# A masked prefix sum and its product on one core: taking the leftover rows behind the first two loads of a round, and transposing the sums in quarters

## The chip, the cores and the metric

The kernel runs on one core of a Trainium2 chip. The metric is the device time of one execution in microseconds (us), as the median of several runs. Most executions agree within a few tenths of a per cent (84.34 to 84.82 us in the fourteen runs of behind_one_warm, below). Some take longer (86.0 us in the profiled run of the kernel before), and a run over 1.5% above the fastest of its kernel is labelled slow.

Ratios are the mean time of one kernel's fast runs over that of the other's from the same rounds, so a ratio is not quite the ratio of the medians quoted beside it.

## The reference

```python
mask = (pos < lengths[:, None, None]).astype(np.float32)
cs = np.cumsum(x * mask, axis=1)              # x: 8 x 8192 x 512, f32
mid_features = cs[b_idx, lengths // 2, :]     # one row for each batch entry
return np.matmul(mid_features[:, None, :], w).squeeze(1)
```

Only one row of the cumulative sum is used, so each batch entry needs the sum of its first min(length, length/2 + 1) rows, times a 512x512 matrix. Those are 570, 2690, 256, 2057, 905, 3772, 3859 and 571 rows. The kernel reads 31.2 MB, hardly more than these rows and `w`.

## The kernel before

The rows are summed by TensorE: a block of 512 rows (128 partitions, four rows each, 1 MB) is multiplied by 0/1 weights and added to PSUM. Whole blocks go through three buffers of two blocks each, the *places* of a round; a round takes three places (two blocks are loaded ahead of the rounds and one, the last, behind them). What is left of each batch entry (fewer than 512 rows) is its *rest*. There are two buffers for rests, and two rests are taken in each of the first four rounds, which are all the rounds that these lengths need. SyncE requests the places' loads, ScalarE the rests' loads, each when the buffer is free again. VectorE prepares the weights of the next round, and only then is a buffer free.

The three pieces that matter, the round on TensorE first:

```python
with pe.Fori(0, rounds):
    with pe.If_cmp(rest_rounds, 1, "IS_GE"):
        for q in range(2):                                  # the two rests of this round
            take(pe, s_rem[q], 16 * (len(PARTS) + 1))       # wait for its loads
            for j in range(G):
                mm = add(j, cur_rem[:, q, j * B:(j + 1) * B], rem[:, q, j])
            mm.then_inc(s_rdone[q], 1)                      # through VectorE, lets ScalarE request the next

    def add_pair(k):
        keep_busy()                                         # three filler matmuls
        take(pe, s_full[k], 32)                             # wait for the place's loads
        ...                                                 # second block, if there is one
        for j in range(G):
            mm = add(j, cur[:, k, 0], xt[:, k, 0, j])
        mm.then_inc(s_done[k], 1)                           # through VectorE, lets SyncE request the next

    pairs(pe, left, add_pair)                               # places 0, 1, 2
```

The fillers (`keep_busy`) are matmuls whose result nobody reads; they are meant to keep TensorE's clock up (in after_cold, below, which has none ahead of the second place, that place of the last round ran at half clock, 3.60 us instead of 1.90). After the last round the sums are copied to SBUF, folded and, with the last block's rows, added up by column (in three pieces, so that the last load is met by little work), transposed by VectorE in two halves, and multiplied by `w`:

```python
for h in range(2):                                          # VectorE
    step(dve.transpose, out=t_sb[:, 2 * h:2 * h + 2].rearrange("p k c -> p (k c)"),
         in_=t_ps[:, :P].rearrange("p (c k) -> p k c", k=KC)[:, 2 * h:2 * h + 2])
...
for kc in range(KC):                                        # TensorE
    if kc % 2 == 0:
        pe.wait_ge(s_dve, DVE_ALL + 3 + kc // 2)
    for j in range(4):
        mm = pe.matmul(o_ps[32 * j:32 * j + B, :P], lhsT=t_sb[:, kc, :B], ...)
```

## Time and profile before

| | before |
|---|---|
| median time | 84.55 us (84.5 to 84.6, 3 runs) |
| the profiled run | 86.0 us, labelled slow |
| span in the profile | 84.1 us |
| read from HBM | 31.23 MB |

The page has a row of digits for each engine: the busy share, in tenths, of each fortieth of the span. The DMA row stands at 9 for nearly the whole kernel, TensorE's (PE) does not. So I take it that the loads set the pace, and that what TensorE does matters only where it delays a load or stands behind the last one. The lines are shown in the prediction; what it calls the ring of an engine are the loads that the engine has requested and that are still to land.

### The profile page before, as it was taken

The numbers are of one execution on the slowest core, as the hardware profiler recorded it, in microseconds if no ns is written. First come the engines' busy times: TensorE is split into PE (matmuls) and PEld (weight loads), VectorE is DVE, ScalarE is ACT, GpSimd is POOL, SyncE is SP. The second block draws the span as 40 slices with busy tenths as digits, with TensorE's granted clock in tenths as the row PEclk, the third lists the DMA queues.
The fourth block names the chain that finished last, engine by engine and source line by source line (L and its number), as shares of the span: only waits on it lengthen the run. The fifth ranks groups of instructions, "written<-read, shape, count | busy, mean of one in ns | idle before, by whom it ended". The sixth has DMA issues, their size and how long they took to land. (4 is left out here: it accounts for less than half of the span.)

```text
span 84.1 us, 1482 instructions
## 1 busy us (share of the span) xinstructions
PE 57.5 (68%) x385; PEld 12.9 (15%) x389; DVE 15.2 (18%) x79; ACT 5.5 (7%) x6; POOL 1.6 (2%) x13
## 2 busy tenths in 40 slices
PE   2950799759980499999406932899979729099730
PEld 2300111112210112121101200111122111023410
DVE  2858887000000000100000010000000000001420
ACT  2991000000000000000000000000000000000020
POOL 6100000000000000000000000000000000000000
PEclk9999999999999555899995696557999999999999
DMA  3799999999999999999999999999999999996000
GB/s 55 288 421 417 441 428 438 445 405 437 417 433 413 421 429 405 421 444 405 452 429 386 441 431 435 398 417 456 415 380 429 429 413 425 402 322 234 6 8 8
DMA packets 3540, 31.26 MB, mean 372 GB/s; under 512 B 531, under 2 KB 547, under 8 KB 1203
## 3 DMA queue, kind: packets, MB, share of 16 engines
q1 hardware_dynamic: 2610, 27.27, 77.5%
q10 hardware_dynamic: 928, 3.97, 12.4%
q8 instruction: 1, 0.02, 0.1%
q14 instruction: 1, 0.00, 0.0%
HBM read 31.23 MB, written 0.02 MB: 372 GB/s over the span
## 5 line engine op out<-in xcount | busy, mean ns | idle before, releaser
L492 PE MATMUL s_ps<-xt,cur 128*8 128x512 f32 x184 | 26.4, 699 | 12.6 <-PEq L146 12.5
L505 PE MATMUL idle_ps<-idle 128*128 128x512 bf16 x44 | 15.3, 443 | 4.0 <-DVE since L340 3.6
L492 PE MATMUL s_ps<-rem,cur_rem 128*8 128x512 f32 x64 | 10.0, 725 | 4.4 <-PEq L146 4.4
L492 PEld LDWEIGHTS s_ps<-xt,cur 128*8 128x8 f32 x184 | 4.3, 95 | 27.7 <-issue 27.7
L456 DVE TENSOR_TENSOR cur<-since 128x16 f32 x9 | 1.7, 187 | 35.6 <-DVEq L146 35.6
L505 PEld LDWEIGHTS idle_ps<-idle 128*128 128x128 bf16 x48 | 3.7, 104 | 21.6 <-issue 20.1
L310 ACT COPY o_sb<-o_ps 8x128 f32<-8x128 f32 x2 | 0.5, 260 | 74.1 <-PE o_ps L586 74.1
L261 ACT ACTIVATE rem<-rem 128x2048 uint32<-128x2048 uint32 x2 | 3.7, 1902 | 0.0
L492 PEld LDWEIGHTS s_ps<-rem,cur_rem 128*8 128x8 f32 x64 | 1.8, 104 | 11.7 <-issue 11.7
L464 DVE COPY cur_rem<-table 128x32 f32 x6 | 1.1, 181 | 11.9 <-DVEq L146 11.9
L516 PE MATMUL s_ps<-zero 1*128 1x512 f32 x2 | 2.1, 1136 | 1.6 <-DVE zero L340 1.6
L340 DVE COPY s_sb<-s_ps 128x256 f32<-128x256 f32 x2 | 0.8, 424 | 12.6 <-PE idle_ps L509 12.6
L492 PE MATMUL s_ps<-first,cur_first 128*8 128x512 f32 x16 | 3.0, 824 | 0.0
L498 PE MATMUL t_ps<-last,e_last 128*8 128x128 f32 x32 | 1.6, 274 | 0.0
L586 PE MATMUL o_ps<-wt,t_sb 128*8 128x128 f32 x32 | 1.1, 273 | 0.5 <-DVE t_sb L340 0.5
L261 ACT ACT_TABLE_LOAD x1 | 1.3, 1283 | 1.4 <-PEq L607 1.4
L340 DVE TENSOR_TENSOR part_a<-since,step_a 1x42 f32<-1x42 f32 (+1 forms) x2 | 1.1, 560 | 0.1
L586 PEld LDWEIGHTS o_ps<-wt,t_sb 128*8 128x8 f32 x32 | 0.8, 89 | 0.7 <-issue 0.7
L340 DVE TENSOR_TENSOR since<-item,begin 1x42 f32<-1x42 int32 (+1 forms) x2 | 0.8, 422 | 0.1
L519 PEld LDWEIGHTS n_ps<-len_f,ones 1*128 1x128 f32 x2 | 0.7, 332 | 1.0 <-DVE len_f L340 0.5
L498 PEld LDWEIGHTS t_ps<-last,e_last 128*8 128x8 f32 x32 | 0.7, 88 | 0.7 <-DMA last<-in_x_dram 0.6
L498 PE MATMUL t_ps<-s_sb,fold 128*8 128x128 f32 x8 | 0.8, 274 | 0.0
(66 smaller groups left out, 13.3 us busy)
## 6 DMA issues: line engine op xcount, KB each, us to landing
xt<-in_x_dram SPq DMA_DIRECT2D x10, 2048.0 KB, 11.7
xt<-in_x_dram SPq DMA_DIRECT2D x3, 1024.0 KB, 10.4
first<-in_x_dram SPq DMA_DIRECT2D x2, 1024.0 KB, 8.0
rem<-in_x_dram ACTq DMA_DIRECT2D x3, 512.0 KB, 8.6
wt<-in_w_dram ACTq DMA_DIRECT2D x1, 1024.0 KB, 4.9
rem<-in_x_dram ACTq DMA_DIRECT2D x3, 256.0 KB, 9.1
last<-in_x_dram SPq DMA_DIRECT2D x1, 512.0 KB, 9.3
last<-in_x_dram SPq DMA_DIRECT2D x2, 256.0 KB, 9.5
```

What stands on the lines that cost most here:

```text
L261: act.memzero(rem[:, q]).then_inc(s_rfree[q], 1)
L310: copy = act.copy(out=o_sb[1][:, j * P:(j + 1) * P], in_=o_ps[64 + 32 * j:64 + 32 * j + B, :P])
L340: do(*args, **kw).then_inc(s_dve, 1)
L456: dve.tensor_tensor(out=cur[:, k], in0=since[:, :B, here].rearrange("p b h -> p h b"), in1=since[:, 1:, here].rearrange("p b h -> p h b"), ...
L464: dve.tensor_copy(out=cur_rem[:, q], in_=rests[:, ds(dve.snap(of, min_val=1, max_val=B // 2 - 1), 1), q].rearrange("p o w -> p (o w)"),).t ...
L492: return pe.matmul(s_ps[32 * j:32 * j + B], lhsT=weights, rhs=rows, start=False, stop=False, skip_group_check=True, tile_position=(0, 32 * j))
L498: return pe.matmul(t_ps[32 * j:32 * j + B, :P], lhsT=weights, rhs=row[:, P * j:P * (j + 1)], start=False, stop=False, skip_group_check=Tru ...
L505: pe.matmul(idle_ps[:], lhsT=idle[:, :P], rhs=idle[:], start=True, stop=True)
L516: pe.matmul(s_ps[:], lhsT=zero[:], rhs=zero[:, :1].to_broadcast((1, D)), start=True, stop=False, skip_group_check=True)
L519: pe.matmul(n_ps[:, :B], lhsT=ones[:], rhs=len_f[:], start=True, stop=True).then_inc(s_pe, 1)
L586: mm = pe.matmul(o_ps[32 * j:32 * j + B, :P], lhsT=t_sb[:, kc, :B], rhs=wt[:, kc, j * P:(j + 1) * P], start=(kc == 0), stop=(kc == KC - 1) ...
```

## The change

Its intent: TensorE shall not stand waiting for rests at the start of a round while the first place has already landed, so that buffers come free earlier; and the product shall start after a quarter of the transposes instead of a half. The diff, cut to its core (VectorE's loop gets the same order):

```diff
         with pe.Fori(0, rounds):
-            with pe.If_cmp(rest_rounds, 1, "IS_GE"):
-                for q in range(2):
-                    take(pe, s_rem[q], 16 * (len(PARTS) + 1))
-                    ...
             def add_pair(k):
                 ...
-            pairs(pe, left, add_pair)
+            pairs(pe, left, add_pair, 0, NS - 1)            # places 0 and 1
+            with pe.If_cmp(rest_rounds, 1, "IS_GE"):
+                for q in range(2):
+                    take(pe, s_rem[q], 16 * (len(PARTS) + 1))
+                    ...
+            pairs(pe, left, add_pair, NS - 1)               # place 2
...
-        for h in range(2):
-            step(dve.transpose, out=t_sb[:, 2 * h:2 * h + 2]..., in_=...)
+        for k in range(KC):
+            step(dve.transpose, out=t_sb[:, k], in_=t_ps[:, :P].rearrange("p (c k) -> p k c", k=KC)[:, k])
...
             for kc in range(KC):
-                if kc % 2 == 0:
-                    pe.wait_ge(s_dve, DVE_ALL + 3 + kc // 2)
+                pe.wait_ge(s_dve, DVE_ALL + 3 + kc)
```

More of the change, by code (lines that the diff above doesn't have):

```diff
@@ L146, in take, with pairs @@
         eng.wait_ge(s, n).then_inc(s, -n)
-    def pairs(eng, n, body, k=0):
-        if k < NS:
+    def pairs(eng, n, body, k=0, most=NS):
+        if k < most:
             with eng.If_cmp(n, 2 * k + 1, "IS_GE"):
                 body(k)
-                pairs(eng, n, body, k + 1)
+                pairs(eng, n, body, k + 1, most)
     def rounds_of(eng, n, least):
@@ L171 @@
     DVE_SEL, DVE_ADDR, DVE_N, DVE_FIRST, DVE_MASK, DVE_ALL = 2, 15, 6, 32, 49, 58
-    DVE_LAST = DVE_ALL + 6
+    DVE_LAST = DVE_ALL + 2 + KC + 2
     PE_ALL, PE_SUM, PE_OUT = 2, 3, 4
@@ L459, in weights @@
                 ).then_inc(s_free[k], 1)
+            pairs(dve, left, weights, 0, NS - 1)
             with dve.If_cmp(rest_rounds, 1, "IS_GE"):
@@ L467, in _ @@
                     ).then_inc(s_rfree[q], 1)
-            pairs(dve, left, weights)
+            pairs(dve, left, weights, NS - 1)
             less(dve, rest_rounds, 1)
@@ L478, in _ @@
         dve.wait_ge(s_pe, PE_SUM)
-        for h in range(2):
-            step(dve.transpose, out=t_sb[:, 2 * h:2 * h + 2].rearrange("p k c -> p (k c)"),
-                 in_=t_ps[:, :P].rearrange("p (c k) -> p k c", k=KC)[:, 2 * h:2 * h + 2])
+        for k in range(KC):
+            step(dve.transpose, out=t_sb[:, k], in_=t_ps[:, :P].rearrange("p (c k) -> p k c", k=KC)[:, k])
         with ending(dve, "dve_last", hint):
@@ L534, in _ @@
         with pe.Fori(0, rounds):
-            with pe.If_cmp(rest_rounds, 1, "IS_GE"):
-                for q in range(2):
-                    take(pe, s_rem[q], 16 * (len(PARTS) + 1))
-                    for j in range(G):
-                        mm = add(j, cur_rem[:, q, j * B:(j + 1) * B], rem[:, q, j])
-                    mm.then_inc(s_rdone[q], 1)
             def add_pair(k):
@@ L550, in add_pair @@
                 mm.then_inc(s_done[k], 1)
-            pairs(pe, left, add_pair)
+            pairs(pe, left, add_pair, 0, NS - 1)
+            with pe.If_cmp(rest_rounds, 1, "IS_GE"):
+                for q in range(2):
+                    take(pe, s_rem[q], 16 * (len(PARTS) + 1))
+                    for j in range(G):
+                        mm = add(j, cur_rem[:, q, j * B:(j + 1) * B], rem[:, q, j])
+                    mm.then_inc(s_rdone[q], 1)
+            pairs(pe, left, add_pair, NS - 1)
             less(pe, left, PER)
```

## The prediction

> **What bounds the kernel now.** I read the page first: the busy tenths by slice, the DMA part and the chain of waits; then the timeline of the last 13 us; then busy times in chosen stretches.
>
> ```profile
> span 84.1 us, 1482 instructions
> ...
> PE   2950799759980499999406932899979729099730
> ...
> PEclk9999999999999555899995696557999999999999
> DMA  3799999999999999999999999999999999996000
> ...
> HBM read 31.23 MB, written 0.02 MB: 372 GB/s over the span
> ...
> DMA 11%; PE 3%; SPq 2%; issue 2%; DVE 1%
> ```
>
> The DMA row is at 9 from the third slice to slice 36, from about 4 to 76 us, while PE has holes all along. The loads bound the kernel; only the last 8 us or so are anything else. So a reordering on TensorE can gain in two ways: if it keeps the load queue from running dry, or if it shortens what comes after the last load. It can lose in one: if it puts work after the last loads.
>
> The end, from the timeline (start us, duration, instruction, idle before it):
>
> ```profile
> 68.01 1.37 SPq L246 DMA_DIRECT2D last<-in_x_dram  x3
> 68.76 1.90 PE L492 MATMUL s_ps<-xt,cur 128*8 128x512 f32 x16 [2.00 <-PEq L146]
> 73.70 1.90 PE L492 MATMUL s_ps<-xt,cur 128*8 128x512 f32 x16 [2.29 <-PEq L146]
> 75.54 0.82 PE L505 MATMUL idle_ps<-idle 128*128 128x512 bf16 x3
> 76.29 1.04 PE L492 MATMUL s_ps<-xt,cur 128*8 128x512 f32 x8
> 77.44 0.88 DVE L340 COPY s_sb<-s_ps 128x256 f32<-128x256 f32 x2 [12.59 <-PE idle_ps L509]
> 78.38 0.39 PE L498 MATMUL t_ps<-s_sb,fold 128*8 128x128 f32 x4
> 78.62 0.41 PE L498 MATMUL t_ps<-last,e_last 128*8 128x128 f32 x8
> 79.09 0.53 DVE L340 STREAM_TRANSPOSE t_sb<-t_ps 128x64 f32<-128x64 f32 x2 [0.77 <-PE t_ps L498]
> 79.49 1.06 PE L586 MATMUL o_ps<-wt,t_sb 128*8 128x128 f32 x32 [0.47 <-DVE t_sb L340]
> ```
>
> These 23 blocks (184 matmul records, eight to a block) make four rounds: three rounds of three places with two blocks each, and a last round of 2, 2 and 1. The reader is to see the last round here: first place at 68.76, second at 73.70 after an idle of 2.29 us, third (one block) at 76.29. Its rests are not in the list, because they were taken earlier, at 64.1, in time in which TensorE would have waited for the first place anyway. After the third place comes a strict sequence: copy of the sums to SBUF, fold, the last rows, transposes, product.
>
> Landings, from issue time plus time to landing: second place 62.14 + 11.2 = 73.3 us; third 65.45 + 10.4 = 75.9; the three pieces of the last rows 77.3 to 78.6. In this run the fold chain and the last landing meet: the fold's matmuls begin at 78.38 and those of the last piece at 78.62. So there is almost no slack between TensorE's sequence behind the second place and the last load.
>
> The profiled run took 86.0 us and counts as slow; the timed ones took 84.5 to 84.6. In its landing events fifteen of the sixteen engine signals of each late load came about 1 us before the sixteenth (last piece: 77.7 against 78.7). I take a fast run to be this one without that laggard: second place landing at 72.3, last piece at 77.7.
>
> [...]
>
> [...] clock 0.5 in stretches of 3.41 or 6.83 us, each after a stretch with little work:
>
> ```profile
> 23.95:27.36 3.41, 0.95 (x7) 0.21 (x3) 0.19 (x1) 0.00 (x0) 0.00 (x0) 0.98 1.03 425
> 27.37:34.20 6.83, 5.78 (x28) 1.11 (x32) 0.37 (x2) 0.00 (x0) 0.00 (x0) 0.51 0.97 411
> 71.74:75.15 3.41, 1.45 (x16) 0.36 (x16) 0.00 (x0) 0.00 (x0) 0.00 (x0) 1.00 0.99 376
> ```
>
> (Stretch, length, busy PE, PE loads, DVE, ACT, POOL, then clock, DMA share, GB/s.) DMA share and rate are the same at half clock: TensorE's speed there did not cost load time.
>
> [...] For the slope I use the trace: 128x256 copies 424 ns, 8x128 copies 280 ns, so 1.1 ns a column.
>
> **The change, part by part.**
>
> 1. In rounds 1 to 3 the rests move behind two places. Work and bytes are unchanged. TensorE frees the first two buffers earlier: in round 1 it waits for rests until 17.79 and takes the first place at 19.52, which had landed at 16.9; in round 3 it stood idle 2.88 us for a rest at 51.9 while the first place had landed at 50.7. The reload of that buffer was issued only at 59.50. That is the thinnest moment: one load (issued 49.32, landed 62.0) was left in the ring. The stretch 60 to 62 us ran at 385 GB/s against 430 before it, so it cost 2 x (1 - 385/430) = 0.2 us. Elsewhere at least a full place of 2 MB, or 4.9 us, was queued. Gain: 0 to 0.2 us, the laggard apart.
>
> 2. In the last round the rests now stand between the second and third places, behind a landing that comes only some 5.3 us before the last one. They are 16 matmul records. At full clock, 16 go in four groups of 0.43 us (loads at 62.37, 62.81, 63.24, then the rests' at 63.66): 1.72 us. From the start of the second place to the start of the last piece's matmuls took 78.62 - 73.70 = 4.92 us; with the rests 6.64 us. In the run as profiled this moves the end by the whole 1.7 us. In a fast run: start at about 72.3 + 0.2 = 72.5, old sequence ready at 77.4, last piece at about 77.6 (0.1 off the stamp, as its matmuls precede it by that); so the new one at 79.1 is 1.5 us later than the load. Cost: 1.5 us, between 1.4 and 1.7.
>
> 3. Transposes in quarters. Now two of 250 ns, starts 0.29 apart, the product starting 0.15 after the first ends. A quarter costs 250 - 32 x 1.1 = 215 ns, starts 0.255 apart: the fourth ends 3 x 0.255 + 0.215 = 0.98 us after the first began, its product starts at 1.13 and its last group (0.107 later) at 1.24. Now that last group starts at 80.25 - 79.09 = 1.16. The first product group comes 0.035 us earlier, but TensorE needs only 0.21 us for a quarter and VectorE 0.255, so the bound passes to VectorE. Cost: 0.05 to 0.1 us instead of a gain.
>
> Sum: 84.55 + 1.5 + 0.05 - 0.2 = 85.9 us. I lower it to 85.8, since earlier reissue may help the loads a little more than the one dip shows.
>
> **The rivals.**
>
> A. The ring's thin moment is worth more than 0.2 us. For it: the laggard first shows in the load after that moment (landing events 66.8 to 68.6), and rests arriving late did block a landed place. Against: the DMA share stays near 1 and fast runs seem not to have the laggard. If earlier issue saves about 1 us in every run, the time is 84.9; if it saves all that part 2 costs, 84.4.
>
> B. The rests of the last round are hidden. It would need over 6.6 us between landings of the second place and the last piece. The third place and the last rows are 2 MB, so about 4.9 us at 425 GB/s plus the slow small pieces, 5.3 in all. Against it, strongly; the sum would then be about 84.5.
>
> C. The rests arrive late at their new place, or the clock is halved at the end. The rests of round 4 are requested after those of round 3 are taken, near 60 us or at half clock up to 63, with up to 5 us of issue time on ACT and 6 to 8.6 us to landing: 70 to 74 us, just ahead of when they are needed (74 us). If late by 1 us: 86.8. Between round 3's third place and round 4's first TensorE now idles some 3 us instead of 2, so half clock becomes likelier there, yet that place is followed by a wait. A halved window over the second place and the rests would add 1.7 us: 87.5; the kernel before has much of the same risk.
>
> **Range and chances.** The middle is 85.8. Low end 84.4, rival A in full; high end 86.8, rival C. The limit for slower is 84.55 x 1.02 = 86.24, inside the upper half; the limit for faster, 82.9, would need the loads to end 1.6 us earlier on a saturated stream. Chances: faster 0.03, same 0.72, slower 0.25.
>
> **What would show it.** Right: in the last 12 us, 16 records on the rests between the second place and the third; copies of the sums starting 5.5 us or more after the second place starts (3.7 now); a gap of about 1.5 us between the landing of the last piece and its matmuls; four transposes of about 0.215 us, and a product that waits between quarters. DMA rates in the middle unchanged. Wrong: last-piece matmuls that still wait for their load, a load stream that ends over 0.5 us earlier, or rests that TensorE waits for in the middle of a round.

## The result, and the profile after

The changed kernel takes 87.48 us in the median of six runs (86.35 to 88.24), against 84.59 before in the same rounds. The ratio of fast runs is 1.0278, with an interval of 1.021 to 1.0346. So it is slower, by 2.9 us in the medians of all runs (2.35 by the ratio of the fast ones) where 1.25 was predicted, and outside the predicted range. The single runs are worth a look: 86.35 and 86.51, then 87.34 and 87.62 (all four labelled fast), and 87.66 and 88.24 (slow). There are two clusters, about 1.1 us apart, and the median lies in the upper one. The profiled run is one of the upper cluster (87.34).

The page after, its first line, the rows of digits and the chain of waits:

```profile
span 85.4 us, 1488 instructions
...
PE   2940899492797707929996470296694922999730
...
PEclk9999999999999999555999999759999997599999
DMA  2799999998999999998999999999999999970000
...
PE 10%; DVE 1%; issue 1%
```

The DMA row is as full as before and ends no later, but four zeros follow it instead of three. The chain that ended last holds no load: it is TensorE nearly all the way. That alone is no difference to the fast state of before, whose chain holds no load either and begins with the second place too (at 72.15 us in before_again, below); the slow profile of before had one. What differs is the length. The first pieces, from the list of the chain in order of time (start us, duration, what), name where it begins:

```profile
71.90 0.22 issue
72.12 4.92 PE s_ps L492 x32
77.04 0.75 PE idle_ps L505 x3
77.79 0.97 PE s_ps L492 x8
```

32 records in a row, 16 for the second place of the last round and 16 for the rests, then the fillers, then the third place. The timeline of the same stretch:

```profile
66.21 1.90 PE L492 MATMUL s_ps<-xt,cur 128*8 128x512 f32 x16 [1.21 <-PEq L146]
72.12 3.20 PE L492 MATMUL s_ps<-xt,cur 128*8 128x512 f32 x16 [3.25 <-PEq L146]
75.14 1.90 PE L492 MATMUL s_ps<-rem,cur_rem 128*8 128x512 f32 x16
77.72 1.04 PE L492 MATMUL s_ps<-xt,cur 128*8 128x512 f32 x8
79.93 0.48 PE L498 MATMUL t_ps<-last,e_last 128*8 128x128 f32 x6
80.46 0.97 DVE L340 STREAM_TRANSPOSE t_sb<-t_ps 128x32 f32<-128x32 f32 x4 [0.71 <-PE t_ps L498]
```

And the kernel before (the run called before_again below):

```profile
68.45 1.90 PE L492 MATMUL s_ps<-xt,cur 128*8 128x512 f32 x16
72.37 1.90 PE L492 MATMUL s_ps<-xt,cur 128*8 128x512 f32 x16 [1.26 <-PEq L146]
75.08 1.04 PE L492 MATMUL s_ps<-xt,cur 128*8 128x512 f32 x8
77.29 0.48 PE L498 MATMUL t_ps<-last,e_last 128*8 128x128 f32 x6
77.82 0.53 DVE L340 STREAM_TRANSPOSE t_sb<-t_ps 128x64 f32<-128x64 f32 x2 [0.71 <-PE t_ps L498]
```

The loads end at nearly the same time in both: by its landing events the last piece is complete at 77.14 us before and 76.97 after. (Landing events, packets and changes of the clock are read from the trace itself and counted from the start of the span, like the timeline. The prediction and the expectations counted theirs from a zero 0.11 us earlier, so those times are 0.11 us too large beside the timeline's.) The transposes start at 77.82 and 80.46, 2.64 us apart. This is the whole loss, and it can be split at the starts of the records:

- The rests take their 1.7 us behind the second place instead of ahead of the first.
- The second place itself takes 75.14 - 72.12 = 3.02 us. At full clock it takes 1.71 (in the order_only run below, 73.80 - 72.09). That is 1.31 us more, and the prediction had left it out of the sum.
- From these 3.0 us come off 0.25 us, as the second place starts at 72.12 instead of 72.37, and about 0.1 us that the third place no longer waits for its load (before, an idle piece of 0.06 us and the end of the fillers ahead of it).

Why was the second place slow? The stretches of 3.41 us between the recorded changes of the clock (length, PE busy, PE loads, VectorE, ScalarE, GpSimd, then the mean granted clock, DMA share, GB/s), in the changed kernel:

```profile
67.97:71.38 3.41, 0.90 (x7) 0.21 (x3) 0.00 (x0) 0.00 (x0) 0.00 (x0) 1.00 0.92 384
71.38:74.79 3.41, 2.67 (x16) 0.62 (x20) 0.00 (x0) 0.00 (x0) 0.00 (x0) 0.50 1.01 413
```

TensorE worked 0.90 of 3.41 us, and for the next 3.41 us its clock was halved: over all of the second place but its end. (In before_again the two stretches up to 73.50 us held 3.41 and 2.15 us of work.) The idle time ahead of the second place had grown from 1.26 us to 3.25, that is by 1.99. The first place landed 1.31 us earlier (65.85 instead of 67.16 us by the landing events), and TensorE took it 0.36 us after its landing instead of 1.29, since no rests stood ahead of it any more; the second place started 0.25 us earlier, having landed at nearly the same time (71.81 and 72.06). What now lands around the gap is the last round's rests: they are requested only after those of the round before were taken, two places later than in the old order, and so they are complete at 68.3 to 72.5 us, where before they were at 60.2 to 65.0. The gap in the old order varies: in the fast profile of quarters_only, below, it is 2.20 us.

### The profile page after: what moved, and what is told of

It is laid out like the page before. It is cut to its first block, busy times and chain, and to the rows that moved or that the text cites.

```text
span 85.4 us, 1488 instructions
## 1 busy us (share of the span) xinstructions
PE 55.4 (65%) x389; PEld 13.0 (15%) x389; DVE 15.6 (18%) x81; ACT 5.5 (6%) x6; POOL 1.6 (2%) x13
## 5 line engine op out<-in xcount | busy, mean ns | idle before, releaser
L492 PE MATMUL s_ps<-rem,cur_rem 128*8 128x512 f32 x64 | 7.8, 593 | 1.5 <-PEq L146 1.5
L340 DVE STREAM_TRANSPOSE t_sb<-t_ps 128x32 f32<-128x32 f32 x4 | 0.9, 216 | 0.8 <-PE t_ps L498 0.7
```

The lines of the kernel that those rows point to most:

```text
L340: do(*args, **kw).then_inc(s_dve, 1)
L492: return pe.matmul(s_ps[32 * j:32 * j + B], lhsT=weights, rhs=rows, start=False, stop=False, skip_group_check=True, tile_position=(0, 32 * j))
```

## The experiments

Fourteen kernels ran, all with correct results.

**before_again** is the kernel before, unchanged.

> The kernel before, unchanged, to get its profile in the fast state and the noise of the comparison. Both theories: 84.5 to 84.7 us, ratio 1.000. If the one late engine signal of the first profile was an accident of the slow run, the last piece lands here about 1 us earlier than there (near 77.7 instead of 78.7 us from the start) with its sixteen signals within 0.5 us. If it belongs to the kernel, it shows again and the time is the same.

Measured: 84.48 us (20 runs), ratio 0.9988 (0.9966 to 1.0011). The last piece lands at 77.14 with its sixteen signals within 0.4 us. So the late signal of the first profile was an accident of that slow run. TensorE's sequence (last matmuls begin at 77.29) and the last load arrive together, so the kernel before has no slack there, as the prediction had it.

**order_only**: the new order with the old two transposes.

```diff
 (the changed kernel)
-        for k in range(KC):
-            step(dve.transpose, out=t_sb[:, k], ...)
+        for h in range(2):
+            step(dve.transpose, out=t_sb[:, 2 * h:2 * h + 2]..., ...)
```

> The new order with the two half transposes of before. Theory: the order is the whole loss, so 86.4 to 87.5 us in two clusters like the changed kernel (ratio 1.02 to 1.035). Rival, the quarters cost something themselves: then this is at least 0.3 us faster than the changed kernel's 87.48.

Measured: 87.67 us (6 runs: 86.62, 87.12, 87.65, 87.69, 87.69, and 88.03, slow), ratio 1.0353 (1.0299 to 1.0407). The order is the whole loss. Its profile fell on the fastest run, at 86.62 us, and shows the other cluster:

```profile
72.09 1.90 PE L493 MATMUL s_ps<-xt,cur 128*8 128x512 f32 x16 [3.52 <-PEq L146]
73.80 1.91 PE L493 MATMUL s_ps<-rem,cur_rem 128*8 128x512 f32 x16
79.14 0.53 DVE L340 STREAM_TRANSPOSE t_sb<-t_ps 128x64 f32<-128x64 f32 x2 [0.71 <-PE t_ps L499]
```

Here the second place runs at full clock, though TensorE was idle even longer ahead of it (3.52 us). The stretches say why:

```profile
66.85:70.26 3.41, 1.72 (x15) 0.25 (x7) 0.00 (x0) 0.00 (x0) 0.00 (x0) 1.00 1.01 426
70.26:73.68 3.42, 1.59 (x16) 0.47 (x20) 0.00 (x0) 0.00 (x0) 0.00 (x0) 1.00 1.00 411
```

In this run the idle time was divided between two stretches, each about half busy, and the clock stayed. In the changed kernel's profile one stretch held nearly all of it. (The limits of these stretches are taken from where the clock changed elsewhere in the same run, in steps of 3.41 us; in the changed kernel's profile the changes lie 6.83, 13.65, 3.41, 13.65, 3.41 and 10.24 us apart, whole multiples of it.) At full clock the transposes start 79.14 - 77.82 = 1.32 us later than before: 1.72 for the rests, less 0.28 for the earlier start of the second place and 0.12 at the third.

**quarters_only**: the old order with four transposes.

```diff
 (the kernel before)
-        for h in range(2):
-            step(dve.transpose, out=t_sb[:, 2 * h:2 * h + 2]..., ...)
+        for k in range(KC):
+            step(dve.transpose, out=t_sb[:, k], ...)
```

> The old order with the transposes in four quarters. Theory: 1.50 us from the first transpose to the copy of the product in the changed kernel against 1.52 us before, so no effect: 84.6 us, within 0.1. Rival: they cost 0.05 to 0.1 us as the prediction worked out, or gain 0.1 us as the change intended.

Measured: 84.65 us (22 runs), ratio 1.0015 (0.9984 to 1.0046): no effect. From the first transpose to the copy of the product it took 79.25 - 77.76 = 1.49 us, against 79.34 - 77.82 = 1.52 in before_again. The intent's gain is not there: four transposes take 0.97 us instead of 0.53, so the product starts 0.04 us earlier and is then paced by VectorE.

**last_ahead**: the changed kernel, but in the last round the rests go ahead of the places again.

```diff
+            with pe.If_cmp(left, PER + 1, "IS_GE"):     # a round follows
                 pairs(pe, left, add_pair, 0, NS - 1)
                 rests()
                 pairs(pe, left, add_pair, NS - 1)
+            with pe.Else():
+                rests()
+                pairs(pe, left, add_pair)
```

> The changed kernel, but in the last round alone the rests stand ahead of the first place again (rounds 1 to 3 keep the new order, and the quarters stay). Theory: the loss comes only from rests standing behind the last round's second place, with its idle and half clock, so it vanishes: 84.0 to 84.7 us. As the rests of the last round are now requested late (near 60 to 65 us) TensorE waits for them until about 72 us before it can take the first place, so some of the loss may stay: first, rests and second then follow in one run, about 72.5 + 1.7 + 1.7 + 1.7 us, which would give 86 us. Rival, the loss comes from the order of the loads in rounds 1 to 3: 86.4 to 87.5 us in any case.

Measured: 92.18 us (6 runs), ratio 1.0834 (1.0755 to 1.0913). Half of my expectation fell, and the doubt written with it was right and still too small. The wait in its timeline:

```profile
73.40 3.28 PE L492 MATMUL s_ps<-rem,cur_rem 128*8 128x512 f32 x16 [7.50 <-PEq L146]
```

TensorE stands for 7.50 us in front of rests that were requested at 63.2 to 69 us. The request of a rest follows the taking of the one before; a new order in one round sets when the next round's rests can be had. The two orders cannot be mixed in this way. Its profile also has one engine signal 1.3 us late, of which more below.

**after_warm**: ten fillers instead of three ahead of the first two places of a round, to take away the idle time.

```diff
-                keep_busy()
+                keep_busy(3 if k == NS - 1 else 10)
```

> The changed kernel with ten filler matmuls instead of three ahead of the first and second places (three, as before, ahead of the third), so that TensorE's idle time between the last round's first and second places falls from about 3.2 to about 1.7 us. Theory, the slower of the two clusters is the halved clock over the second place (3.02 us instead of 1.71 in the changed kernel's profile): all runs go to the faster cluster, 86.2 to 86.6 us. Rival, the clusters come from the loads (a late engine, the order on the rings): the median stays near 87.5 us.

Measured: 87.53 us (6 runs), ratio 1.0327 (1.0291 to 1.0363); all five fast runs at 87.39 to 87.60. It reads as a win for the rival, but the profile shows that another loss had come in. The clock was full in the last round, the second place took 1.71 us, and yet it started at 73.72 us, because the last of its sixteen engine signals came at 73.41; the fifteenth had come at 71.80. The late engine is there from a load that landed near 27 us on. At 26.13 us the trace has one packet of 16 KB on the queue of kind "instruction". The kernels so far that were fast have none between 6 and 80 us.

**after_nofill**: the changed kernel without fillers ahead of the third place.

```diff
-                keep_busy()
+                keep_busy(0 if k == NS - 1 else 3)
```

> The changed kernel without the three filler matmuls ahead of the third place. Theory, after the second place's landing TensorE's own sequence sets the end and the last load has landed long before: the fillers' 0.75 us come off in full, so about 86.7 us in the median (85.6 to 85.8 in runs at full clock). Rival, the last loads still set the end: no change, 87.5 us.

Measured: 86.81 us (85.03, then 86.78 to 86.82 four times, and 87.68). The four are labelled slow only because they are over 1.5% above the one at 85.03, so there is no ratio to speak of. By clusters, 86.8 stands against 87.3 to 87.6 of the changed kernel. Its profile is of the cluster with half clock over the second place, like the changed kernel's: from the start of that place to the transposes 79.80 - 72.13 = 7.67 us, against 80.46 - 72.12 = 8.34. The fillers' time comes off (0.87 us between the end of the rests and the third place is gone; the second place was 0.2 us slower in this run). So TensorE's own sequence sets the end, and not the last load, which had landed at 77.0 in both. The run at 85.03 is faster than the 85.6 to 85.8 expected of a run at full clock; it has no profile.

**last_behind**: the old order, but in the last round the rests stand behind the second place.

```diff
 (the kernel before)
+            with pe.If_cmp(left, PER + 1, "IS_GE"):
                 rests()
                 pairs(pe, left, add_pair)
+            with pe.Else():
+                pairs(pe, left, add_pair, 0, NS - 1)
+                rests()
+                pairs(pe, left, add_pair, NS - 1)
```

> The kernel before, but with the rests behind the second place in the last round only. Rests of that round are then requested as early as before and have landed long ago; its first place is taken near 67.5 to 68.5 us, so that TensorE is idle for less than 2.5 us ahead of the second and the clock should stay full in most runs. Theory: the rests' 1.72 us less what slack there was (0.1 to 0.4 us): 85.9 to 86.3 us. Rival, the whole loss is made by what rounds 1 to 3 do to the loads: 84.6 us.

Measured: 88.03 us (6 runs), ratio 1.0369 (1.032 to 1.0419), so well above what I had expected. From the start of the second place to the transposes it took 81.28 - 74.23 = 7.05 us, as in order_only (79.14 - 72.09 = 7.05), so the rests' 1.7 us are there, with the loads of rounds 1 to 3 in their old order. But the second place started only at 74.23: again one engine signal was late (73.92 against 72.05), again after a 16 KB packet of instructions, here at 32.29 us. The code of a round is in this program twice, so it is longer.

**behind_one**: the rests behind the first place instead of two.

```diff
 (the changed kernel, on TensorE; the same on VectorE)
-            pairs(pe, left, add_pair, 0, NS - 1)
+            pairs(pe, left, add_pair, 0, 1)
             ... the rests ...
-            pairs(pe, left, add_pair, NS - 1)
+            pairs(pe, left, add_pair, 1)
```

> The changed kernel with the rests behind the first place instead of the first two. Theory: in the last round they fill idle time ahead of the second place's landing, so nothing is added behind it and the clock has no reason to fall: 84.3 to 84.7 us, equal to before (the stream of loads sets the end there). Rival, rests requested one place later than before come too late for this place, as they did in the run with the last round's rests ahead: 86 us or more.

Measured: 85.46 us (17 runs; the fast ones four at 84.59 to 84.69, ten at 85.09 to 85.67), ratio 1.0061 (1.0031 to 1.0091). Most of the loss is gone. In the profile (84.69 us) the rests stand in what had been idle time:

```profile
67.45 1.90 PE L492 MATMUL s_ps<-xt,cur 128*8 128x512 f32 x16 [3.51 <-PEq L146]
69.16 1.91 PE L492 MATMUL s_ps<-rem,cur_rem 128*8 128x512 f32 x16
```

The 3.51 us of idle time are now ahead of the first place, which suggested half clock over the first place and the rests as the reason for the runs near 85.4.

**after_warm2** does over again what after_warm was meant for, without a longer program: three f32 fillers ahead of the second place, and three fillers ahead of the loop left out.

```diff
-        keep_busy()
+        pe.wait_ge(s_pool, 3)                 # the f32 tile of ones is there
         pe.wait_ge(s_dve, DVE_MASK)
...
-                keep_busy()
+                keep_warm(3) if k == 1 else keep_busy()
```

> The changed kernel with three f32 filler matmuls (about 2.5 us) instead of three bf16 ones (0.8 us) ahead of the second place; three fillers ahead of the loop are left out, so TensorE's program is no longer than the changed kernel's. Theory: the slower cluster of the changed kernel is half clock over the last round's second place, and what kept the earlier run with ten fillers slow was one DMA engine made late by an instruction fetch (16 KB at 26.24 us) that its longer program needed. So here: no fetch in mid-run, full clock in the last round, 86.2 to 86.6 us in nearly all runs. Rival, the second cluster has another cause: median stays near 87.5.

Measured: 86.9 us (fast runs 86.24, 86.33, 86.49, 87.31; slow ones 87.61 and 88.38), ratio 1.0257 (1.0212 to 1.0302). No packet of instructions in mid-run; in its profile (86.33) the clock is full from 54.9 us to the end of the work. So there are now more runs in the lower cluster, but not all: not settled by this run.

**before_long**: the kernel before with ten fillers in the first two places.

> The kernel before with ten fillers instead of three ahead of the first and second places: the old order, but the longer program of the earlier run with ten fillers. Theory: a 16 KB fetch of instructions falls into the stream of loads, one of sixteen engine signals is 1.3 to 1.8 us late from then on, and the time is 85.3 to 86.2 us although TensorE's order has not changed. Rival, a longer program costs nothing and the late engine was chance: 84.4 to 84.7 us.

Measured: 86.89 us (86.12 to 87.82), ratio 1.0238 (1.0195 to 1.0282). The packet is there (25.69 us) and so is the late signal (0.85 us), but the time does not measure them. The fillers had cost time as well: TensorE reached the second place of the last round at 75.09 us, 2.0 us after its last signal at 73.10. The test was badly made; before_dead takes its place.

**behind_one_warm**: behind_one with three f32 fillers ahead of the first place.

```diff
-                keep_busy()
+                keep_warm(3) if k == 0 else keep_busy()
```

> Rests behind the first place, with the three f32 fillers ahead of the first place and a program of the same length. Theory: the runs of the rests-behind-one kernel at 85.1 to 85.7 us had half clock over the last round's first place and rests (TensorE idle 3.5 us ahead of them), and go to 84.4 to 84.7 us. Rival, they come from the order itself: median stays near 85.4.

Measured: 84.49 us (14 runs, 84.34 to 84.82), ratio 0.9995 (0.9977 to 1.0013). The cluster near 85.4 is gone, and the kernel is as fast as the one before, not faster. Its second place starts at 72.49 us and its transposes at 77.82.

**after_warm3**: four f32 fillers ahead of the second place.

> The changed kernel with four f32 fillers (about 3.5 us) ahead of the second place, and six fillers ahead of the loop left out for them. TensorE's idle time ahead of the last round's second place falls below 1 us. Theory, the slower cluster is half clock there: all fast runs at 86.2 to 86.7 us, and none at 87.3 to 87.7. Rival, the cluster comes from elsewhere, as one run at 87.31 us with three f32 fillers may say: about half of the runs stay at 87.3 or more.

Measured: 87.39 us (fast runs 86.26, 86.44, 87.36, 87.41; slow ones 87.56 and 87.69), ratio 1.0241 (1.0165 to 1.0316). Still two clusters. The profiled run (87.41) had full clock over the second place, but TensorE came late to it: halved clock from 60.0 to 66.9 us had made it late at the places before, and 3.7 us of fillers followed.

```profile
69.86 3.70 PE L512 MATMUL idle_ps<-idle 128*128 128x512 f32 x8
73.49 1.90 PE L494 MATMUL s_ps<-xt,cur 128*8 128x512 f32 x16
```

The place had landed at 72.06. Fillers against a falling clock can thus bring the same loss themselves. As a test it is inconclusive.

**before_dead**: the kernel before with fourteen filler matmuls that are jumped over and never run.

```diff
         keep_busy()
+        with pe.If_cmp(left, 1000, "IS_GE"):
+            keep_busy(14)
         pe.wait_ge(s_dve, DVE_MASK)
```

> The kernel before with fourteen filler matmuls that are jumped over and never run, ahead of the loop: what is executed stays the same but for one compare, the program is as long as in the runs with ten fillers. Theory: instructions are fetched in mid-run by one 16 KB packet, one engine signal is 1 to 2 us late from there to the end, and the time is 85.2 to 86.2 us. Rival, the fetch costs nothing or does not come because the code is not run: 84.4 to 84.7 us.

Measured: 85.85 us (six runs, 85.71 to 85.93), ratio 1.0141 (1.0096 to 1.0186). Code that never runs costs 1.2 us by the ratio (1.35 by the medians). The DMA queues between 31 and 35 us:

```profile
q1 hardware_dynamic: 201, 1.56, 94.2%
q8 instruction: 1, 0.02, 1.7%
```

That one packet starts at 32.19 us. From the load that lands next (32.79 us for fifteen signals, 34.35 for the sixteenth) to the last piece (77.02 and 78.34) the sixteenth signal stays at least 1.3 us behind. So the last piece is complete 1.2 us later than in before_again (77.14), which is what the kernel lost.

**after_cold** tests the clock the other way round, with less work: no fillers ahead of the second place.

```diff
-                keep_busy()
+                keep_busy(0 if k == 1 else 3)
```

> The changed kernel without the three fillers ahead of the second place of a round (all others stay). It does less work, and TensorE's idle time ahead of the last round's second place grows from 3.2 to about 4 us. Theory, half clock over that place makes the slower cluster: now every run has it, so all fast runs are at 87.2 to 87.8 us and none at 86.2 to 86.6; its profile shows about 3.0 to 3.4 us for the second place's sixteen matmuls. Rival, the clusters have nothing to do with TensorE's idle time: again a mix, or faster.

Measured: 87.76 us (fast runs 87.54, 87.64, 87.68, 87.76, 87.85 and 88.63, a slow one at 89.0), ratio 1.036 (1.0308 to 1.0413). There is no run in the lower cluster any more. The profile (of the run at 88.63) has the place and the rests behind it at half clock:

```profile
72.08 3.60 PE L492 MATMUL s_ps<-xt,cur 128*8 128x512 f32 x16 [4.17 <-PEq L146]
75.45 3.01 PE L492 MATMUL s_ps<-rem,cur_rem 128*8 128x512 f32 x16
```

Seven runs without one in the lower cluster would be weak evidence alone: with two in six, as in the changed kernel, chance gives that about once in 17. Together with behind_one_warm (fillers in, and the upper cluster goes: 14 runs of 14 against 4 of 14 fast ones) and with the stretches of all the profiles (the last section) it shows that too little work of TensorE in one stretch makes the clusters. What the single runs without a profile had is inferred from their times.

## Why the prediction was wrong, point by point

**What bounds the kernel.** Right. The loads bound the kernel before, and TensorE's sequence behind the second place of the last round has no slack against the last load; before_again shows both (last matmuls from 77.29 us, last piece complete at 77.14). That the stream of loads could go no faster was my assumption: in the first profile of before the slices 3 to 35 of the page ran at 380 to 456 GB/s, and no run tests whether that is a limit.

**Part 1, rounds 1 to 3 (gain 0 to 0.2 us).** Right in size: the last piece lands 0.17 us earlier (76.97 against 77.14). One of its signs of being wrong did come, rests that TensorE waits for in the middle of a round: in round 3 it waited 1.53 us for the second rest, until 60.62 us; the last loads ended no later for it. Rival A, a gain of about 1 us from a fuller ring, did not happen; the late engine signal that spoke for it was an accident of the slow run.

**Part 2, the last round's rests (cost 1.4 to 1.7, taken as 1.5).** The mechanism was right, and its size nearly: 1.32 us at full clock in order_only, and 79.46 - 77.82 = 1.64 in after_warm2. The two fast runs of the lower cluster, 86.35 and 86.51, are this part and some 0.4 to 0.6 us more: their spans (84.1 and 84.2 us) are 1.3 and 1.4 us longer than before_again's 82.8, and the rest lies outside the span, where the trace shows nothing (86.35 - 84.1 = 2.25 us, against 1.8 in most runs of before_again and 84.79 - 82.8 = 1.99 in the profiled one).

**Part 3, the quarters (cost 0.05 to 0.1).** The single operation was right (216 ns measured, 215 worked out), the sign was not: 0.03 us of gain from transpose to copy, nothing in the time. The step that failed is the hand-over to the last quarter's product. I had let each quarter's product wait 0.15 us after its transpose, as the first one does; the last record of the product ends at 79.18 us, 0.45 us after the fourth transpose (ended 77.76 + 0.97 = 78.73), where 0.15 + 0.107 + 0.273 = 0.53 had been counted.

**Rival C, the clock (named at 1.7 us, and given little weight).** This is where the prediction failed. It said that TensorE would idle longer between round 3's third place and round 4's first, "yet that place is followed by a wait", and that a halved window over the second place was a risk that "the kernel before has much of" as well. In fact the late rests land mostly between the first and the second place, and no longer stand ahead of the first, so the idle time that grew was the one ahead of the second place, where nothing behind is a wait: 3.25 us against 1.26 in the fast run of before, 2.20 in quarters_only and 2.29 in the slow run of before. I had the numbers for it: I had put the rests' landing at 70 to 74 us and did not draw the conclusion that the first place, which now lands before them, would land earlier (65.85 us instead of 67.16) and the second hardly (71.81 and 72.06). The term missing from the sum is 1.31 us (3.02 us instead of 1.71). Rival C's own figure, 87.5 us, is the measured time by luck in part: it stood for 1.5 + 1.7, where the spans show 1.32 + 1.31 and the rest lies outside them; and the range ended at 86.8, without it. By the times, the term comes in most runs and not in all. The two profiles show what it depends on, where the clock's stretches of 3.41 us fall: the changed kernel's stretch ahead of the second place held 0.90 us of work and half clock followed, and the two of order_only held 1.72 and 1.59 and the clock stayed full.

In spans, 82.8 + 1.3 gives the lower cluster's 84.1, and another 1.3 the profiled run's 85.4 of the upper one, which holds the median. The chance of 0.25 for slower was too low for the same reason.

**The clock in the trace of before.** The stretches that the prediction shows had what was needed: 0.95 us of work in 3.41 us (1.06 with the limits 0.11 us earlier), and for the next 6.83 us a clock of 0.51. The changed kernel's profile agrees (0.90 us of work in 3.41 us, then clock 0.50). The prediction applied it to the wrong gap.

Not settled: why the time outside the span is some 0.4 us longer in those two runs (2.52 us in the run of order_only at 86.62, but 1.8 to 1.9 in the three lower runs of after_warm2), and why after_warm2 kept runs in the upper cluster. No profile fell on one of the latter; after_warm3 suggests TensorE made late by its fillers.

## What to carry to other kernels

In this kernel, bound by its loads, the rests on TensorE were free where they stood ahead of a landing (behind_one_warm: ratio 0.9995), and cost most of their length behind the last landing that they could not overlap (order_only: 1.72 us of them, and the transposes 1.32 us later); before moving such work, see which side of the last two landings it comes to stand on. If a buffer's next request follows the taking of its content, a later taking moves the next load as well, and with it the gaps between the landings around it (here the last round's rests were complete at 68.3 to 72.5 us instead of 60.2 to 65.0, and the idle time ahead of the second place was 3.25 us instead of 1.26). And a gap ahead of work on the path to the end can bring that work to half clock (3.02 us instead of 1.71 for the second place). In these traces that took a stretch of 3.41 us with less than about 1.4 us of work, so a gap of little over 2 us was enough where it fell into one stretch (2.24 us ahead of the last round's first place in last_behind, which then took 3.25 us instead of 1.90), and one of 3.52 us did no harm where it was divided between two.

## What the traces show of instruction packets, the clock and VectorE

- In before_dead one packet of 16 KB (1.06 us long, at 32.19 us) passes on the queue of kind "instruction" while the loads run. Each load gives sixteen engine signals; from the next load on the sixteenth stayed at least 1.3 us behind, to the end, and the fourteen matmuls that were never run made the kernel 1.4% slower (85.85 us, ratio 1.0141). Four other programs, which were longer because they held a round twice or more fillers, show the same packet and the same late signal:

```
kernel         16 KB of instructions at   last piece, sixteenth signal after fifteenth
before_again   84.08 us (after the work)  0.04 us
after          82.64 us (after the work)  0.01 us
before_dead    32.19 us                   1.32 us
after_warm     26.13 us                   1.38 us
before_long    25.69 us                   0.85 us
last_behind    32.29 us                   1.83 us
last_ahead     30.53 us                   1.31 us
```

Such a packet is not the only thing that comes before a late signal: in the slow first profile of before the last piece's sixteenth signal was 0.95 us late, and its only 16 KB packet (81.58 us) came after the work.

- The limit of work below which the clock fell is narrow. The clock's recorded changes give the limits of the windows of 3.41 us, and the profiles TensorE's busy time (here: work) in each. Over all sixteen profiles, from the first record of the clock on, the 46 windows at full clock with up to 1.30 us of work in 3.41 were all followed by half clock, and the 202 with 1.46 us or more by full clock; of the four between, those with 1.34 and 1.40 us stayed and those with 1.35 and 1.45 fell. (The prediction's windows lie 0.11 us late; in their place, its first and third have 1.06 and 1.34 us.)
- VectorE's 128x64 transpose took 250 ns in the first profile of before and its 128x32 one 216 ns in quarters_only: half the elements, and 34 ns less. Of four quarters instead of two halves no gain came (0.97 us against 0.53 for all the transposes). The 128x256 copies from PSUM to SBUF took 424 ns.
